# SSD group norm: column sums on four 32-column tiles, a small root and reciprocal, and a broadcast through device memory

## The chip, the cores and the metric

The program runs on one core of a Trainium2 chip. The metric is device time in microseconds (us), from the first to the last instruction with a little around it; the median of three runs is 1379.9 us (1378.26 to 1380.02). Engines: PE (matrix products), ACT, DVE and POOL (elementwise), SP (only issues transfers).

## The reference, cut to what matters

Two layers on 512 tokens of width 1024: a gated short convolution and a Mamba-2 SSD mixer, each followed by a SwiGLU feed-forward. The change lies in the group norm near the end of the SSD mixer: 2048 channels in 8 groups of 256, each token normalised within its group.

```python
def ssd_mixer(h, ...):
    z, xbc, dt_raw = jnp.split(h @ w_in, [M_D_INNER, M_D_INNER + M_CONV_DIM], axis=-1)
    xbc = jax.nn.silu(causal_depthwise_conv(xbc, conv_w) + conv_b)
    ...
    y = ssd_chunked(xs, dt, a, bm, cm) + d_skip.reshape(g, r)[:, :, None] * xs
    y = y.reshape(bsz, s, M_D_INNER) * jax.nn.silu(z)
    y = rms_normalize(y.reshape(bsz, s, g, M_D_INNER // g)).reshape(bsz, s, M_D_INNER) * norm_g
    return y @ w_out
```

`rms_normalize` divides by the root of the mean square plus 1e-6.

## The kernel before

Activations lie transposed, channels on the 128 partitions and the 512 tokens along the row, so one SSD group is two tiles of 128x512. Everything is float32; the large products split each operand into a rounded high part and a low rest and run three products (`mm3`, L259 to L261: high x high, high x low, low x high). `load_w` loads a weight block into `wst`, ACT casts the high part into `whl` (L202) and DVE subtracts to get the low part (L203). There are four `whl` buffers. One projection of 128 columns (`in_chunk`, tile `ip`) is 24 products of 512 columns.

The SSD layer is a software pipeline over the 8 groups. Pass g of the loop (called stage g here, g = 1 to 7) runs the recurrence of group g while it projects group g+1. In code order a stage is:

- projection 1 of group g+1; `step_a` of group g: transposes `xtok` and `btokp`, products `cb`; on DVE `xw`, `xdt` and `cbm`
- projection 2; `step_b`: the states (`st01` at L1051, `st2` at L1053, then `prev` on DVE) and the decays `csb` (exponential on ACT at L1073, multiplication on DVE at L1074)
- projections 3 and 4; `step_cc`: the outputs `yo` and `yd`, gated and squared into `accg`
- two projections for the gate z; then `step_d`, the group norm that is changed

A projection is followed by `conv4`: ACT starts the accumulator `cu` (L954), DVE adds three shifted terms (L957, three instructions), and ACT applies SiLU (L959). In stage 7 there is nothing left to project, and PE begins the output projection (`y`) instead.

The order on PE is the code's, by hand. On DVE, ACT, SP and POOL a scheduler lays the instructions of the loop into one fixed order per engine when the program is built; each engine then works strictly in that order, and an instruction that waits holds up everything behind it. The end of stage g−1 (`step_d` of group g−1) is finished during stage g.

`step_d` before: with a 128x128 matrix of ones PE adds the squares over the partitions, which leaves the same sum in all 128 rows of `ssg`; ACT takes the root of the 128x512 tile `rg` (L1119), DVE its reciprocal (L1120), and two DVE products scale the two tiles `yg` (L1123), in place. The readers of `yg` come later: `y_act` (L1133, L1134) splits it into `ys` for the output projection. `aux_ps` tiles come from one ring of four PSUM buffers in code order, so `st2` takes the buffer that the second `xtok` tile had, once both `xw` and `xdt` have read it. `bt` has two buffers; group g+2 writes the one that group g had.

Of the kernel before, what the change touches and what calls it, by code (L numbers as in the profile page):

```python
# [8 lines left out]
F32 = mybir.dt.float32  # L9
F32R = mybir.dt.float32r  # L10
AF = mybir.ActivationFunctionType
# [5 lines left out]
P = 128  # L17
# [8 lines left out]
NG = 8  # L26
NCH = 4
# [8 lines left out]
def trunk_kernel(  # L36
# [9 lines left out]
    act, dve, pe, pool = nc.scalar, nc.vector, nc.tensor, nc.gpsimd  # L46
# [3 lines left out]
    dram = ctx.enter_context(tc.tile_pool(name="dram", bufs=1, space=DRAM))  # L50

    tmp = ctx.enter_context(tc.tile_pool(name="tmp", bufs=4))
# [7 lines left out]
    def aux_ps(name, shape=(P, T)):  # L60
        return ps.tile(list(shape), F32, tag="aux", name=name, bufs=4)

    def t2(name):
        return tmp.tile([P, T], F32, tag="t2", name=name, bufs=4)
# [4 lines left out]
    ones = consts.tile([P, P], F32, name="ones")  # L69
# [3 lines left out]
    eps_t = consts.tile([P, 1], F32, name="eps")  # L73
# [791 lines left out]
    with ExitStack() as ph:  # L865
# [4 lines left out]

        cs_d = dram.tile([NH, T], F32, name="cs_d")
        ecs_d = dram.tile([NH, T], F32, name="ecs_d")

        dt_tok = consts.tile([P, NH, NCH], F32, name="dt_tok")
        cs_tok = consts.tile([P, NH, NCH], F32, name="cs_tok")
# [89 lines left out]
        class Group:  # L965
# [147 lines left out]
            def step_d(self):  # L1113

                g = self.g
                pt = aux_ps("ssg")
                pe.matmul(pt, ones, self.accg, start=True, stop=True)
                rg = t2("rg")
                act.activation(rg, pt, AF.Sqrt, bias=eps_t, scale=1.0 / 256)  # L1119
                dve.reciprocal(rg, rg)  # L1120
                for q in range(2):
                    y = ygs[2 * g + q]
                    dve.scalar_tensor_tensor(y, y, mng[:, 2 * g + q:2 * g + q + 1], rg, MUL, MUL)  # L1123
# [394 lines left out]
```

## Time and profile before

| | |
|---|---|
| median of three runs | 1379.9 us |
| the profiled execution | 1378.87 us, span 1377.0 us |
| granted TensorE clock, mean over the span | 0.994 |
| ACT busy, POOL busy | 580.2 us (42%), 1.5 us |
| one `ssg` product (L1117), x16 (two passes for each of 8 groups) | 591 ns as recorded |
| root of `rg` (L1119), x8 | 688 ns |
| reciprocal of `rg` (L1120), x8 | 3352 ns |
| scaling of `yg` (L1123), x16 | 745 ns |
| transfers issued by POOL | none |

Columns of the trace's rows: start in us, length in us, engine, line, operation, operands, count, and in brackets the idle time before it with what ended it. PE's records overlap, so what a product costs is read from start to start, not from its length.

### The profile page before, as it was taken

How to read it: one execution, taken by the hardware profiler on the slowest of the kernel's cores; microseconds unless marked ns; L12 is line 12 of the kernel's file. 1: busy time of each engine (PE TensorE's matmuls, PEld its weight loads, DVE VectorE, ACT ScalarE, POOL GpSimd, SP SyncE). 2: the span in 40 equal slices, each digit the busy share in tenths (PEclk: the TensorE clock that was granted, in tenths of full speed). 3: DMA queues.
4: the chain of work that ended last, by engine and by line, in shares of the span. 5: the costliest groups of instructions: out<-in, count | busy, mean ns of one | idle time of the engine just before them, and what ended most of it. 6: DMA issues, size and time to landing. Idle time of an engine off the chain costs nothing.

```text
span 1377.0 us, 17627 instructions
## 1 busy us (share of the span) xinstructions
PE 1353.4 (98%) x6973; PEld 1136.3 (83%) x6973; DVE 911.3 (66%) x1485; ACT 580.2 (42%) x875; POOL 1.5 (0%) x11
## 2 busy tenths in 40 slices
PE   8999999999999999999899999999999999999997
PEld 7788889888888888898778888888889888887886
DVE  5777757478775222669879888787675655334877
ACT  4432247222222211665655656543473222223754
POOL 0000000000000000000000000000000000000000
PEclk9999999999999999999989999999999999999999
DMA  9956670467683322514444324332233986423743
GB/s 314 318 182 218 228 238 24 136 215 274 215 283 106 130 93 69 149 33 144 120 139 128 91 89 138 108 107 92 92 122 134 343 276 244 134 69 128 249 163 118
DMA packets 163702, 222.09 MB, mean 161 GB/s; under 512 B 7060, under 2 KB 112164, under 8 KB 161188
## 3 DMA queue, kind: packets, MB, share of 16 engines
q1 hardware_dynamic: 159616, 208.20, 46.2%
q10 hardware_dynamic: 4004, 12.77, 2.9%
q8 instruction: 55, 0.90, 0.3%
q14 instruction: 27, 0.22, 0.0%
HBM read 207.17 MB, written 13.78 MB: 160 GB/s over the span
## 4 chain that ended last, share of the span: by engine, by line
PE 63%; DVE 3%; DMA 1%; ACT 0%; issue 0%; DVEq 0%; ACTq 0%
PE ip L259 11%; PE ip L261 11%; PE ip L260 11%; PE y L359 5%; PE y L360 5%; PE y L361 5%; PE li L259 2%; PE li L261 2%; PE li L260 2%; PE yd L1089 1%; PE yo L1082 1%; PE pa L1390 1%; PE pa L1391 1%; PE pb L1391 1%; PE pb L1390 1%; PE pb L1389 1%
## 5 line engine op out<-in xcount | busy, mean ns | idle before, releaser
L259 PE MATMUL ip<-h,whl 128*128 128x512 f32 x1096 | 434.6, 397 | 2.7 <-DVE cv L777 2.7
L261 PE MATMUL ip<-h,whl 128*128 128x512 f32 x1096 | 429.4, 392 | 6.6 <-DVE whl L203 6.6
L260 PE MATMUL ip<-h,whl 128*128 128x512 f32 x1096 | 428.4, 391 | 0.0
L261 PEld LDWEIGHTS ip<-h,whl 128*128 128x128 f32 x1096 | 206.8, 189 | 50.9 <-DVE whl L203 7.0
L259 PEld LDWEIGHTS ip<-h,whl 128*128 128x128 f32 x1096 | 206.8, 189 | 47.7 <-issue 5.1
L260 PEld LDWEIGHTS ip<-h,whl 128*128 128x128 f32 x1096 | 206.9, 189 | 43.3 <-issue 1.2
L202 ACT CAST whl<-wst 128x1024 fp32r<-128x1024 f32 (+1 forms) x163 | 152.2, 952 | 200.7 <-PE ip L261 148.2
L203 DVE TENSOR_TENSOR whl<-wst,whl 128x1024 fp32r<-128x1024 f32 (+1 forms) x163 | 177.0, 1102 | 62.4 <-ACT whl L202 62.0
L203 DVE TENSOR_TENSOR whlo<-wsto,whlo 128x1024 fp32r<-128x1024 f32 x46 | 56.3, 1224 | 96.2 <-ACT whlo L202 96.0
L126 DVE SCALAR_TENSOR_TENSOR ada_acc<-ada_st,csil,ada_acc 128x512 f32<-128x512 f32 x140 | 104.8, 749 | 22.6 <-DMA ada_st<-in_ada_w_dram 19.7
L202 ACT CAST whlo<-wsto 128x1024 fp32r<-128x1024 f32 x46 | 48.3, 1050 | 113.8 <-PE y L361 86.7
L259 PE MATMUL li<-h,whl 128*128 128x256 f32 x288 | 83.2, 289 | 0.0
L261 PE MATMUL li<-h,whl 128*128 128x256 f32 x288 | 81.6, 283 | 0.0
L260 PE MATMUL li<-h,whl 128*128 128x256 f32 x288 | 81.5, 283 | 0.0
L957 DVE SCALAR_TENSOR_TENSOR cu<-ip,cols,cu 128x511 f32<-128x511 f32 (+2 forms) x84 | 62.0, 741 | 12.9 <-ACT cu L954 12.7
L359 PE MATMUL y<-whlo,ff 128*128 128x512 f32 x176 | 68.6, 390 | 0.0
L361 PE MATMUL y<-whlo,ff 128*128 128x512 f32 x176 | 68.5, 389 | 0.0
L360 PE MATMUL y<-whlo,ff 128*128 128x512 f32 x176 | 68.5, 389 | 0.0
L259 PEld LDWEIGHTS li<-h,whl 128*128 128x128 f32 x288 | 55.3, 192 | 0.0
L260 PEld LDWEIGHTS li<-h,whl 128*128 128x128 f32 x288 | 55.2, 192 | 0.0
L261 PEld LDWEIGHTS li<-h,whl 128*128 128x128 f32 x288 | 55.1, 191 | 0.0
L359 PE MATMUL y<-whlo,ys 128*128 128x512 f32 x128 | 51.1, 399 | 0.0
(281 smaller groups left out, 1923.5 us busy)
## 6 DMA issues: line engine op xcount, KB each, us to landing
ada_st<-in_ada_w_dram SPq DMA_DIRECT2D x96, 512.0 KB, 5.9
wst<-in_f_w_in_dram SPq DMA_DIRECT2D x44, 1024.0 KB, 7.1
wst<-in_m_w_in_dram SPq DMA_DIRECT2D x14, 1024.0 KB, 5.4
tb<-in_f_w_out_dram SPq DMA_DIRECT2D x22, 512.0 KB, 7.3
td<-tb SPq DMA_DIRECT2D x11, 1024.0 KB, 5.0
wsto<-in_f_w_out_dram SPq DMA_DIRECT2D x10, 1024.0 KB, 4.9
wst<-in_m_w_in_dram SPq DMA_DIRECT2D x20, 512.0 KB, 5.1
wst<-in_a_w_in_dram SPq DMA_DIRECT2D x9, 1024.0 KB, 6.5
```

The costliest lines, as they stand in the source:

```text
L126: dve.scalar_tensor_tensor(acc, w, csil[:, k:k + 1], acc, MUL, ADD)
L202: act.copy(dst[:, 0, :nk, :], src)
L203: dve.tensor_tensor(dst[:, 1, :nk, :], src, dst[:, 0, :nk, :].bitcast(F32), SUB)
L259: pe.matmul(dst, w_at(w, 0, kk), a[:, 0, sl], start=start, stop=False)
L260: pe.matmul(dst, w_at(w, 0, kk), a[:, 1, sl], start=False, stop=False)
L261: pe.matmul(dst, w_at(w, 1, kk), a[:, 0, sl], start=False, stop=stop)
L359: pe.matmul(pst, a[:, 0, tk], wt[:, 0, kk, :], start=k == 0, stop=False)
L360: pe.matmul(pst, a[:, 0, tk], wt[:, 1, kk, :], start=False, stop=False)
L361: pe.matmul(pst, a[:, 1, tk], wt[:, 0, kk, :], start=False, stop=k == K - 1)
L957: dve.scalar_tensor_tensor(u[:, sft:], pst[:, :T - sft], w[3 - sft], u[:, sft:], MUL, ADD)
L1390: pe.matmul(acc[t], a[:, 0, sl], w[1], start=False, stop=False, skip_group_check=True)
L1391: pe.matmul(acc[t], a[:, 1, sl], w[0], start=False, stop=True, skip_group_check=True)
```

## The change

`ssg` becomes a 128x128 tile. Four products, one for each 128 tokens, each use 32 columns of the ones matrix and write their own 32 rows, on four column tiles of the array. The root and the reciprocal then work on 128x128 (tile `r4`) in place of 128x512. Four rows of it, one for each 128 tokens, are stored to device memory as 512 numbers, and a second transfer reads them back into all 128 partitions. Both transfers are issued by POOL. The landing place is the group's own `bt` tile, so `rg` no longer takes one of the four `t2` buffers.

```diff
+        rg_d = [dram.tile([NCH, P], F32, name=f"rg_d{g}") for g in range(NG)]
...
             def step_d(self):
                 g = self.g
-                pt = aux_ps("ssg")
-                pe.matmul(pt, ones, self.accg, start=True, stop=True)
-                rg = t2("rg")
-                act.activation(rg, pt, AF.Sqrt, bias=eps_t, scale=1.0 / 256)
-                dve.reciprocal(rg, rg)
+                pt = aux_ps("ssg", (P, P))
+                for cc in range(NCH):
+                    pe.matmul(pt[cc * 32:(cc + 1) * 32, :], ones[:, :32], self.accg[:, cc * P:(cc + 1) * P],
+                              start=True, stop=True, tile_position=(0, cc * 32))
+                r4 = tmp.tile([P, P], F32, tag="r4", name="r4", bufs=1)
+                act.activation(r4, pt, AF.Sqrt, bias=eps_t, scale=1.0 / 256)
+                dve.reciprocal(r4, r4)
+                pool.dma_start(rg_d[g], r4[0:P:32, :])
+                rg = self.bt
+                pool.dma_start(rg, rg_d[g].rearrange("c t -> (c t)").partition_broadcast(P))
                 for q in range(2):
                     y = ygs[2 * g + q]
                     dve.scalar_tensor_tensor(y, y, mng[:, 2 * g + q:2 * g + q + 1], rg, MUL, MUL)
```

The order on PE stays as it was, with four products of 128 columns where one of 512 stood; lines after the change move down by one to six. The scheduler lays DVE and ACT out anew from stage 1 to the end of the SSD layer. DVE in stage 1 before, from the two `yg` products to the first weight split (`whl`, for projection 3); the reciprocal stands two rows ahead of the first row, and the split for projection 4 two rows behind the last:

```order
L1123 SCALAR_TENSOR_TENSOR yg_5432<-yg_5432,cols_89,rg 128x512
L1123 SCALAR_TENSOR_TENSOR yg_5440<-yg_5440,cols_89,rg 128x512
L957 SCALAR_TENSOR_TENSOR cu<-ip,cols_91,cu 128x510
L957 SCALAR_TENSOR_TENSOR cu<-ip,cols_91,cu 128x511
L957 SCALAR_TENSOR_TENSOR cu<-ip,cols_91,cu 128x509
L957 SCALAR_TENSOR_TENSOR cu<-ip,cols_91,cu 128x510
L1056 TENSOR_TENSOR prev<-prev,dec 128x256
L957 SCALAR_TENSOR_TENSOR cu<-ip,cols_91,cu 128x509
L1058 TENSOR_TENSOR prev<-prev,st_5629 128x256
L1074 TENSOR_TENSOR csb<-csb,cbm 128x1024
L1056 TENSOR_TENSOR prev<-prev,dec 128x256
L203 TENSOR_TENSOR whl<-wst,whl 128x1024
```

DVE at the same place in the changed kernel, where the reciprocal stands three rows ahead of the first row; the last row is the split for projection 4:

```order
L958 SCALAR_TENSOR_TENSOR cu<-ip,cols_91,cu 128x509
L1075 TENSOR_TENSOR csb<-csb,cbm 128x1024
L203 TENSOR_TENSOR whl<-wst,whl 128x1024
L1129 SCALAR_TENSOR_TENSOR yg_5440<-yg_5440,cols_89,bt 128x512
L1129 SCALAR_TENSOR_TENSOR yg_5448<-yg_5448,cols_89,bt 128x512
L958 SCALAR_TENSOR_TENSOR cu<-ip,cols_91,cu 128x511
L1057 TENSOR_TENSOR prev<-prev,dec 128x256
L958 SCALAR_TENSOR_TENSOR cu<-ip,cols_91,cu 128x510
L1059 TENSOR_TENSOR prev<-prev,st_5642 128x256
L958 SCALAR_TENSOR_TENSOR cu<-ip,cols_91,cu 128x509
L1057 TENSOR_TENSOR prev<-prev,dec 128x256
L203 TENSOR_TENSOR whl<-wst,whl 128x1024
```

The first split moved from ten rows behind the `yg` products to the row ahead of them; the second stays behind them, with three `cu` and three `prev` instructions between. Both `yg` now read `bt`, so they wait for the second transfer.

DVE in stage 2 of the changed kernel (stages 3 to 6 differ in that both `xdt`, `cbm` and a second `cu` stand ahead of `yg`):

```order
L1123 RECIPROCAL r_5853<-r_5853 128x128
L203 TENSOR_TENSOR whl<-wst,whl 128x1024
L1024 TENSOR_TENSOR xw<-xtok,dte_tok 128x512
L1026 TENSOR_TENSOR xdt<-xtok,dt_tok 128x512
L958 SCALAR_TENSOR_TENSOR cu<-ip,cols_91,cu 128x511
L1024 TENSOR_TENSOR xw<-xtok,dte_tok 128x256
L1129 SCALAR_TENSOR_TENSOR yg_5769<-yg_5769,cols_89,bt 128x512
L1129 SCALAR_TENSOR_TENSOR yg_5777<-yg_5777,cols_89,bt 128x512
L958 SCALAR_TENSOR_TENSOR cu<-ip,cols_91,cu 128x510
L1026 TENSOR_TENSOR xdt<-xtok,dt_tok 128x512
```

In stage 2 the second `xdt` stands behind the two `yg`, as it did before; what moved ahead of them is a weight split, the first `xdt` and one `cu`. POOL, which had no transfers, now issues these, in pairs, and nothing else stands between them:

```order
L566 MEMSET rows 128x256
masks.py:66 AFFINE_SELECT mask<-mask 128x128
L1124 DMA rg_d_4976<-r_5523 4x128
L1126 DMA bt<-rg_d_4976 128x512
L1124 DMA rg_d_4977<-r_5853 4x128
L1126 DMA bt<-rg_d_4977 128x512
```

`rg_d` is the group's tile in device memory. On POOL the second transfer of a pair waits for the landing of the first.

## Prediction

> **What bounds the kernel.** I read the first part of the page, then the windows view cut at stages of the SSD layer, the chain of waits for the distance from one stage to the next, and the timeline of PE and DVE where a stage is longer.
>
> ```profile
> PE 1353.4 (98%) x6973; PEld 1136.3 (83%) x6973; DVE 911.3 (66%) x1485; ACT 580.2 (42%) x875; POOL 1.5 (0%) x11
> 680.00:720.00 40.00, 33.42 (x164) 27.05 (x163) 32.44 (x54) 23.20 (x28) 0.00 (x0) 0.87 0.40 119
> 720.00:760.50 40.50, 40.50 (x217) 33.77 (x216) 34.87 (x59) 23.77 (x30) 0.00 (x0) 1.00 0.39 117
> 670.13 0.86 PE ssg L1117 x2
> 719.27 0.86 PE ssg L1117 x2
> 759.73 0.86 PE ssg L1117 x2
> ```
>
> PE is busy 1353.4 of 1377.0 us: what PE doesn't execute, or doesn't wait for, is the gain. The windows rows (stage 1, stage 2: length, then PE busy) show stage 2 full, 40.50 of 40.50, and stage 1 with 33.42 of 40.00 at a mean clock of 0.87. By the chain, `ssg` follows `ssg` after 719.27 − 670.13 = 49.1 us in stage 1 and after 759.73 − 719.27 = 40.5 in stage 2. So stage 1 loses 8.6 to 8.7 us, taken as 8.7.
>
> ```profile
> 684.56 0.39 PE L260 MATMUL ip<-h,whl 128*128 128x512 f32 x1
> 691.53 0.79 PE L261 MATMUL ip<-h,whl 128*128 128x512 f32 x1 [6.58 <-DVE whl L203]
> 692.12 0.63 PE L259 MATMUL ip<-h,whl 128*128 128x512 f32 x1
> 696.81 0.61 PE L261 MATMUL ip<-h,whl 128*128 128x512 f32 x1
> 697.96 0.39 PE L259 MATMUL ip<-h,whl 128*128 128x512 f32 x1
> 703.40 0.39 PE L259 MATMUL ip<-h,whl 128*128 128x512 f32 x1
> 678.54 1.23 DVE L1074 TENSOR_TENSOR csb<-csb,cbm 128x1024 f32<-128x1024 f32 x1
> 679.68 3.35 DVE L1120 RECIPROCAL rg<-rg 128x512 f32<-128x512 f32 x1
> 683.51 1.41 DVE L1123 SCALAR_TENSOR_TENSOR yg<-yg,cols,rg 128x512 f32<-128x512 f32 x2
> 684.84 2.71 DVE L957 SCALAR_TENSOR_TENSOR cu<-ip,cols,cu 128x510 f32<-128x510 f32 x4
> 690.25 1.22 DVE L203 TENSOR_TENSOR whl<-wst,whl 128x1024 fp32r<-128x1024 f32 x1
> 678.93 1.98 ACT L202 CAST whl<-wst 128x1024 fp32r<-128x1024 f32 x2
> ```
>
> PE (first six rows) stops in projection 3: the third product waits 6.58 us for the low part of a weight block. Then eleven steps from 692.12 to 696.81 take 0.43 us each, where the 24 from 697.96 to 703.40, a whole projection in 5.44 us, take 0.227. DVE (next five) is late with that split (690.25) because by its order the reciprocal (3.35 us), two `yg` and two convolutions come first, though ACT (last row) had cast both blocks of the pair by 680.9.
>
> **The products.** The same shape, 128 rows by 32 columns, 128 moving columns, float32 on four column tiles, runs at the start of the kernel, between full-width products. One float32 product has two records.
>
> ```profile
> 19.72 0.40 PE L714 MATMUL li<-h,whl_b 128*128 128x512 f32 x1
> 20.05 1.08 PE L184 MATMUL ada_pe<-ada_st,rows 128*32 128x128 f32 x32
> 21.06 0.96 PE L714 MATMUL li<-h,whl_b 128*128 128x512 f32 x3
> 31.38 1.95 PE L184 MATMUL ada_pe<-ada_st,rows 128*32 128x128 f32 x64
> 33.26 0.44 PE L191 MATMUL ada_pe<-ident,ada 128*128 128x128 f32 x2
> 706.26 1.90 PE yd L1089 x32
> 708.15 0.43 PE ip L259
> ```
>
> Start to start, 32 records take 21.06 − 20.05 = 1.01 us and 64 take 1.88: 0.027 a record, plus 0.14 that doesn't scale. A further 0.1 stands ahead of the group, which starts 0.33 behind the product at 19.72, not 0.23. Eight records then cost 8 × 0.027 + 0.24 = 0.46 us, where the two passes of the old `ssg` cost 0.86 by the chain: −0.40, eight times −3.2 us. The outer ends: −5.2 if entering and leaving the tiles costs nothing (8 × 0.65), and +1.9 if the four don't overlap (0.86 + 0.24 each).
>
> The rows of `yd`, two 64-column tiles, show the cost of leaving: the product behind them takes 0.43 in the chain, 0.2 more than the pitch. The Trainium skill (TensorEngine Tiling, Key Properties) says that changing the tiling mode drains the engine, which speaks against four small products between full ones; the row agrees. By that page's up-to-fourfold speedup alone `ssg` would fall to a quarter, the −5.2 end, and the sum would be 2 us lower than with the drain.
>
> **Root and reciprocal.**
>
> ```profile
> L935 ACT ACTIVATE csb<-csb 128x128 f32<-128x128 f32 x1 | 0.3, 311 | 0.7 <-DVE csb L933 0.7
> L908 DVE RECIPROCAL cs_tok<-cs_tok 128x128 f32<-128x128 f32 x1 | 1.0, 952 | 0.0
> 721.61 0.69 ACT L1119 ACTIVATE rg<-ssg,eps 128x512 f32<-128x512 f32 x1
> 762.98 0.69 ACT L1119 ACTIVATE rg<-ssg,eps 128x512 f32<-128x512 f32 x1
> ```
>
> On 128x128, ACT takes 0.31 us (an exponential of that size, row one) where the root takes 0.69 (the last two rows, stages 2 and 3), and DVE 0.95 where the reciprocal took 3.35. That is 3 us of ACT and 19 us of DVE in all, but off PE's path except in stage 1, so it counts only there. Elsewhere I cost it at nothing: PE's own work covers it, full in stage 2. Without that cover the 19 us would show in full.
>
> **The two transfers.** POOL waits for the reciprocal, issues the store, waits for its landing, issues the load; DVE waits for that at the first `yg`, with everything behind it in its order. Call R the time from the end of the reciprocal to the landing. No row shows a transfer issued by POOL; the nearest are these (KB, median us from issue to landing), and the share of the transfer engines is zero at both places where R runs.
>
> ```profile
> out_dram<-x SPq DMA_DIRECT2D x8, 256.0 KB, 2.0
> cs_d<-csb SPq DMA_DIRECT2D x1, 64.0 KB, 3.1
> ea<-in_m_a_log_dram SPq DMA_DIRECT2D x1, 16.0 KB, 2.8
> r<-td SPq DMA_DIRECT2D x11, 256.0 KB, 3.5
> ecsb<-ecs_d ACTq DMA_DIRECT2D x16, 256.0 KB, 5.9
> 680.00:684.00 4.00, 4.00 (x20) 3.35 (x19) 4.00 (x3) 1.67 (x2) 0.00 (x0) 1.00 0.00 0
> 720.00:724.00 4.00, 4.00 (x19) 3.29 (x18) 1.67 (x1) 3.95 (x5) 0.00 (x0) 1.00 0.00 0
> ```
>
> The store lies between 2.0 (an output tile) and 3.1 (also a table to device memory); the load between 2.8 (a small broadcast) and 5.9 (256 KB broadcast, but queued behind 1 MB). With idle engines I take the upper store, the quiet 256 KB load at 3.5 and 0.4 for two hand-overs: R = 7.0. Ends: 4.8 and 9.0, and above it what POOL may add.
>
> **Stage 1 with the new order.** PE is 0.4 earlier by the shorter `ssg`, and so is DVE, which waits for PE ahead of this place. The reciprocal starts at 679.68 − 0.4 = 679.3 and ends at 680.2. Three `cu` (0.66 each), one `csb` (1.14, from 678.54 to 679.68) and the split (1.13: its 1.22 less the 0.09 by which DVE's records overlap) end at 684.5. PE asks for it at 684.56 + 0.23 − 0.4 = 684.4: the 6.58 us are gone but for 0.1. That removes 8.7 − 0.1. What is late next is the split for projection 4. Behind `yg` (1.33, from 683.51 to the row at 684.84) come three `cu`, three `prev` (0.34 each) and the split, so it ends at 680.2 + R + 1.3 + 2.0 + 1.0 + 1.1 = 685.6 + R. PE asks 24 products later: 684.5 + 5.44 = 690.0. The wait is R − 4.4, or 2.6 us at R = 7.0. The weights of the z projections are split behind that and needed two projections later.
>
> A wait of that size also halves the clock:
>
> ```profile
> 64.39 0.47 PE L259 MATMUL ip<-h,whl 128*128 128x512 f32 x1 [2.69 <-DVE cv L777]
> 65.87 0.63 PE L259 MATMUL ip<-h,whl 128*128 128x512 f32 x1
> 68.86 0.56 PE L260 MATMUL ip<-h,whl 128*128 128x512 f32 x1
> ```
>
> After 2.69 us idle the seven products from 65.87 to 68.86 took 0.43 each, a loss of about 1.6 us with the next. I add 1.6 for a wait near 2.6 and 2.6 for one above 5 (thirteen slow products at 691.53); under 2 nothing. Stage 1 then gains 8.7 − 0.1 − 2.6 − 1.6 = 4.4 us; at R = 4.8 it gains 8.2, at 9.0 some 2.0 (wait 4.6, clock 2.0).
>
> **The other stages.**
>
> ```profile
> 733.89 0.59 PE L1053 MATMUL st<-xw,btok 128*128 128x256 f32 x2
> ```
>
> In stage 2 the root ends at 721.61 + 0.31 and the reciprocal at 722.8 (0.09 of it overlapped). `yg`, one `cu` and the second `xdt` end at 725.4 + R, and `st2`, in that `xdt`'s PSUM buffer, starts at 733.89 + 0.15 − 0.4: hidden to R = 8.2. In stages 3 to 6 (root from 762.98, so the reciprocal ends at 764.2) the next that PE needs behind `yg` is the split for projection 4: `cu`, two `csb` and it end at 769.6 + R; PE asks 20.8 us after `ssg` at 759.73, an estimate from stage 2 (`st2` ends at 734.5, projection 3 takes 5.44). Hidden to R = 10.9. `bt` is wanted by the group after next, some 20 us later, and stage 7 works ahead by up to five `ys` buffers; both count as nothing. The kernel's end keeps its distance, since PE is full behind the layer.
>
> **Sum.** Products −3.2, stage 1 −4.4, transfers elsewhere 0: −7.6 against the profiled 1378.87: 1371.3. The median of the runs is 1.0 above that execution, so 1372.3; I forecast 1372.
>
> **Rivals** (by the median, with −3.2 for the products).
>
> - A short trip, R = 4.8: the split for projection 4 is 0.4 late, the clock holds, 1379.9 − 3.2 − 8.2 = 1368.5. Idle transfer engines speak for it, the wait of one engine on another twice over against. The Trainium skill (DMA: Bandwidth & Descriptors, Anatomy of one DMA) gives about 2.0 us a transfer plus bytes at 436 GB/s: 4.6 us for the pair, an estimate, so this case; no row here shows a POOL transfer.
> - A trip above 11 us, and slower: then `yg` holds DVE in every stage. At R = 12.5, stage 1 loses 8.1 + 2.6 against the prize of 8.7, stage 2 loses 4.3 and stages 3 to 6 lose 1.6 each: 8.7 − 10.7 − 0.1 − 4.3 − 6.4 + 3.2 = −9.6, so 1389. It decides from R = 11, where the sum is near zero. The longest row is 5.9 + 3.1 = 9.0; POOL would have to add 2 us.
> - A trip of 9 to 11: stage 1's gain shrinks to nothing and stage 2 waits up to 2.8 us: 1376 to 1380.
> - The four products don't run side by side: +1.9 in place of −3.2, 1377.4. The rows at 20.05 speak against it.
>
> **Numbers.** Forecast (R from 5.5 to 9, 1369 to 1376) 0.55; short trip 0.22; 9 to 11 us 0.10; above 11 us 0.09; no overlap of the products 0.04. A measurement of this kernel tells about 0.2% (2.8 us) from no change, so faster means below 1377.1. Faster is the first two and a third of the third: 0.80, less 0.02 for what I don't see, 0.78; same 0.11 from the rest of the third and the last; slower 0.11. The range from 1366 to 1380 takes in the short trip with the upper end of the products (1368.5 − 2.0) and the trip of 11 us.
>
> **What would show it.** Right: the wait of PE for `whl` at projection 3 is gone and a shorter one, 1 to 5 us, stands at projection 4 of stage 1 with a half-clock stretch behind it; `ssg` near 0.46 us in the chain; stages of 40.1 us; DVE idle at `yg` for the transfer in every stage. Wrong: R far from 7 (read from the reciprocal's end to `yg`), PE waits in stages 2 to 6, or `ssg` at 0.9 us.

## The result, and the profile after

| | before | after |
|---|---|---|
| median of six runs each | 1379.96 us | 1372.32 us (1368.89 to 1373.76) |
| the profiled execution, span | 1378.87, 1377.0 us | 1371.87, 1370.1 us |

The ratio is 0.9943, with a 95% interval from 0.9931 to 0.9955: 7.6 us faster, against a forecast of 1372. The total came out as forecast; the terms did not, and the rest of this document explains why.

First the page of the changed kernel, PE's busy row and the group that carried the wait, then the chain of waits, its rows for `ssg` (stages 1, 2, 3 and the last):

```profile
PE 1349.0 (98%) x7021; PEld 1133.1 (83%) x7021; DVE 894.9 (65%) x1485; ACT 577.3 (42%) x875; POOL 10.8 (1%) x27
L261 PE MATMUL ip<-h,whl 128*128 128x512 f32 x1096 | 428.0, 391 | 1.6 <-DVE whl L203 1.5
...
671.18 0.36 PE ssg L1119 x8
712.64 0.36 PE ssg L1119 x8
752.78 0.36 PE ssg L1119 x8
...
958.96 0.36 PE ssg L1119 x8
```

PE waits 1.5 us for `whl` in place of 6.6. Stage 1 is 712.64 − 671.18 = 41.46 us (before 49.14), stage 2 40.14 (before 40.46). From the first `ssg` to the last it is 287.78 us, before 298.01 (670.13 to 968.14): the layer gained 10.2 us, not the forecast 7.6. Ahead of it this execution was 1.05 us later (in 13 profiles of all kernels here the first `ssg` starts anywhere from 668.7 to 671.2, so that is chance). Behind it, it lost: 1370.1 − 958.96 = 411.1 us against 408.9. The sum is −10.2 + 1.05 + 2.3 = −6.9, the difference of the two spans.

Stage 1 of the changed kernel, by the timeline of DVE, POOL and PE:

```profile
680.41 0.95 DVE L1123 RECIPROCAL r<-r 128x128 f32<-128x128 f32 x1
681.27 2.22 DVE L958 SCALAR_TENSOR_TENSOR cu<-ip,cols,cu 128x511 f32<-128x511 f32 x3
683.41 1.22 DVE L1075 TENSOR_TENSOR csb<-csb,cbm 128x1024 f32<-128x1024 f32 x1
684.54 1.22 DVE L203 TENSOR_TENSOR whl<-wst,whl 128x1024 fp32r<-128x1024 f32 x1
687.43 1.42 DVE L1129 SCALAR_TENSOR_TENSOR yg<-yg,cols,bt 128x512 f32<-128x512 f32 x2 [1.68 <-DMA bt<-rg_d]
...
691.74 1.22 DVE L203 TENSOR_TENSOR whl<-wst,whl 128x1024 fp32r<-128x1024 f32 x1
681.68 0.71 POOL L1124 DMA_DIRECT2D rg_d<-r  x1 [679.59 <-DVE r L1123]
684.04 0.56 POOL L1126 DMA_DIRECT2D bt<-rg_d  x1 [1.65 <-PE ip L261]
685.81 0.50 PE L261 MATMUL ip<-h,whl 128*128 128x512 f32 x1
693.00 0.50 PE L261 MATMUL ip<-h,whl 128*128 128x512 f32 x1 [1.46 <-DVE whl L203]
693.34 0.39 PE L259 MATMUL ip<-h,whl 128*128 128x512 f32 x1
693.57 0.39 PE L260 MATMUL ip<-h,whl 128*128 128x512 f32 x1
```

The split for projection 3 (684.54) now stands behind the short reciprocal, three `cu` and one `csb`, and PE goes on at 685.81, some 0.3 us late. The trip R runs from 681.36 to `yg` at 687.43: 6.07 us. The split for projection 4 (691.74) comes behind it, and PE waits 1.46 us. Behind that wait the steps are 0.34 and then 0.23 us: the clock was not halved.

The end of the program, before and after: the chain's row for the first load of the last FFN, and PE's products behind it.

```profile
1258.91 4.83 DMA r<-td
```
```profile
1249.27 5.04 DMA r<-td
1255.43 0.50 PE L1395 MATMUL pb<-w,a 128*128 128x512 f32 x1 [0.75 <-ACT w L1330]
1256.69 0.56 PE L1396 MATMUL pb<-w,a 128*128 128x512 f32 x1 [0.76 <-DVE w L1331]
1257.05 0.63 PE L1397 MATMUL pb<-w,a 128*128 128x512 f32 x1
1257.48 0.63 PE L1395 MATMUL pb<-w,a 128*128 128x512 f32 x1
...
1260.04 0.57 PE L1395 MATMUL pz<-w,a 128*128 128x512 f32 x1
```

The load lands 0.2 us later, two waits of 0.75 us follow (0.54 and 0.76 before), and then seven steps of 0.43 us. From the first `pa` product to the end the program took 116.9 us, before 114.2. Of these 2.7 us, 0.2 are the load and 1.2 the slow steps. Another 1.2 lie behind PE's last product, which starts 7.4 us ahead of the end before and 8.6 after. The order of the instructions of this stretch is the same in both kernels on every engine.

### The profile page after: what moved, and what is told of

It is laid out like the page before. It is cut to its first block, busy times and chain, and to the rows that moved or that the text cites. A ratio compares the mean times of both kernels' runs of the same rounds, so it can differ in the third digit from the quotient of the medians.

```text
span 1370.1 us, 17791 instructions
## 1 busy us (share of the span) xinstructions
PE 1349.0 (98%) x7021; PEld 1133.1 (83%) x7021; DVE 894.9 (65%) x1485; ACT 577.3 (42%) x875; POOL 10.8 (1%) x27
## 4 chain that ended last, share of the span: by engine, by line
PE 64%; DVE 2%; DMA 1%; ACT 0%; issue 0%; SPq 0%; DVEq 0%; ACTq 0%
PE ip L259 11%; PE ip L261 11%; PE ip L260 11%; PE y L359 5%; PE y L361 5%; PE y L360 5%; PE li L259 2%; PE li L261 2%; PE li L260 2%; PE yd L1090 1%; PE yo L1083 1%; PE pb L1396 1%; PE pb L1397 1%; PE pz L1395 1%; PE pz L1397 1%; PE pz L1396 1%
## 5 line engine op out<-in xcount | busy, mean ns | idle before, releaser
L202 ACT CAST whlo<-wsto 128x1024 fp32r<-128x1024 f32 x46 | 48.4, 1051 | 113.6 <-PE y L361 86.8
```

Source lines behind the costliest of these rows:

```text
L202: act.copy(dst[:, 0, :nk, :], src)
```

## Experiments

The kernels ran in three groups (four, four and the three shifts), each on one chip beside the kernel before, whose medians were 1378.79, 1378.96 and 1378.69 us. Stage 1 is the distance of the first two `ssg` in the profiled execution.

| | median, us | ratio to before, 95% interval | stage 1, us |
|---|---|---|---|
| after_again | 1370.31 | 0.9941 [0.9928, 0.9954] | 41.62 |
| order_only | 1374.33 | 0.9969 [0.9956, 0.9981] | 46.40 |
| order_after | 1368.58 | 0.9925 [0.9913, 0.9937] | 39.30 |
| full_sums | 1378.33 | 0.9992 [0.998, 1.0003] | 48.98 |
| order_full | 1374.82 | 0.9967 [0.995, 0.9983] | 42.04 |
| quarter_recip | 1375.56 | 0.9976 [0.9965, 0.9987] | 45.69 |
| long_trip | 1372.70 | 0.9951 [0.9934, 0.9968] | 42.33 |
| double_products | 1368.64 | 0.9914 [0.9894, 0.9935] | 40.66 |
| shift_before | 1381.47 | 1.002 [1.0008, 1.0033] | 48.62 |
| shift_after | 1369.51 | 0.9929 [0.991, 0.9949] | 41.60 |
| shift_best | 1365.66 | 0.9906 [0.9887, 0.9925] | 39.28 |

**What gained in stage 1: the order on DVE, or less work for it?**

order_only, the old arithmetic with another order. `step_e` is the second half of `step_d` (reciprocal and `yg`; the other groups still run it there), `splits` lists DVE's weight splits as they are written, and `issue_after` lets an engine issue what stands in its block only after the instruction named:

```diff
...
+                    if g == 1 and i == 2:       # in the loop, behind projections 3 and 4
+                        with tc.issue_after(splits[-1].ins):
+                            first.step_e()      # group 0: reciprocal and yg
```

> The kernel before, with the old sums, root and reciprocal; only in stage 1 DVE's reciprocal and the two scalings of group 0 are queued behind both weight splits of projections 3 and 4. PE's order and the order of SP's transfers stay as before. Theory 'order' (the 8.7 us of stage 1 were the place of the split behind 3.35 us of reciprocal and what followed it): no wait of PE for whl in stage 1, the distance from ssg to ssg there 40.5 us instead of 49.1, 1379.96 - 8.6 = 1371.4 us, so as fast as the changed kernel. Theory 'work' (DVE must have less to do: 2.4 us less reciprocal in each stage): the delayed reciprocal only moves the wait to a later projection, stage 1 stays at 46 to 49 us, 1377 to 1380 us.

```profile
688.04 3.35 DVE L1129 RECIPROCAL rg<-rg 128x512 f32<-128x512 f32 x1
...
700.88 1.22 DVE L205 TENSOR_TENSOR whl<-wst,whl 128x1024 fp32r<-128x1024 f32 x1
702.15 0.79 PE L263 MATMUL ip<-h,whl 128*128 128x512 f32 x1 [3.95 <-DVE whl L205]
```

My theory 'order' fell as I had put it. The waits at projections 3 and 4 are gone, but 3.95 us stand at the first z projection, whose split (700.88) is behind the delayed reciprocal, `yg` and step c. Stage 1 is 46.40, within what 'work' said; the median, 1374.33, lies between what the two theories said (1371.4, and 1377 to 1380). So I took the z split ahead as well, order_full:

```diff
...
+                        if g == 1 and q == 2:
+                            with tc.issue_after(splits[-1].ins):
+                                first.step_e()
+                    if g == 1 and i == 2:
+                        nxt.weights(2)
+                        with tc.issue_after(splits[-2].ins):
+                            step()              # step_cc behind the first z split
```

> The kernel before with its old sums, root and reciprocal, as in order_only, and in stage 1 also the first z split taken ahead of step c on DVE (in order_only PE waited 3.95 us for that split, which stood behind the delayed reciprocal, the scalings and step c). Theory 'order' (DVE's work fits into stage 1, only its order is at fault): the z split ends near 697.9, PE asks at 698.2, no wait of PE for whl; stage 1 39.6 us (39.30 of order_after plus 0.32 for the products), 1378.8 - 9.5 - 0.6 = 1368.7 us. Theory 'work' (old reciprocals don't fit, 4.7 us of reciprocal and scalings must show somewhere): a wait of 2 us or more appears at the end of stage 1 (ssg for accg, or the next xtok), stage 1 43 us or more, 1372 us or more.

```profile
712.83 1.10 PE L1119 MATMUL ssg<-accg,ones 128*128 128x512 f32 x2 [2.17 <-DVE accg L1112]
714.04 0.63 PE L262 MATMUL ip<-h,whl 128*128 128x512 f32 x1
```

The wait for `whl` shrank to 0.2 us, and 2.17 us came up at the end of the stage, `ssg` for `accg`, with half-clock steps (0.43) behind it: the place that 'work' named. Stage 1, 42.04, fits neither theory's number (39.6, and 43 or more); the median, 1374.82, fits 'work'. Stages 1 and 2 together took 84.34 us. Without waits they would take 39.30 (order_after) + 0.32 (the dearer products) + 40.46 = 80.1, so order alone brought 5.2 of the 9.5 us that stage 1 had lost, and the other order that I tried, order_only, brought less there (86.86 us for the two stages). The medians of the two fell by 4.5 and 4.1, order_only's more. Then less work alone, quarter_recip, which leaves the other three quarters of `rg` without a reciprocal:

```diff
-                dve.reciprocal(rg, rg)
+                dve.reciprocal(rg[:, :P], rg[:, :P])
```

> The kernel before, with the reciprocal taken of only the first 128 of 512 columns (the other three quarters are left as the root): DVE has 2.4 us less in each stage, and no transfer moves the scalings back. By its order the split for projection 3 still stands behind the scalings, six cu, one csb and three prev: 679.7 + 0.9 + 1.3 + 4.0 + 1.1 + 1.0 + 1.1 = 689.2 against 691.4 before. Theory 'order': the wait of PE falls from 6.6 to 4.4 us only, stage 1 46.8 us, 1378.8 - 2.3 - 0.6 = 1375.9 us. Theory 'work' (the shorter reciprocal carries the gain): wait under 1 us, stage 1 near 41 us, 1371 us.

```profile
690.07 0.50 PE L261 MATMUL ip<-h,whl 128*128 128x512 f32 x1 [4.20 <-DVE whl L203]
```

A wait of 4.20 us where the sum of what stands ahead of the split gave 4.4, and a median of 1375.6 where it gave 1375.9. Stage 1, 45.69, is 1.1 below the 46.8 that I had said. Size alone brings 49.14 − 45.69 = 3.4 us. And the trip alone, with old sums and old reciprocal, full_sums:

```diff
+                pt = aux_ps("ssg")
+                pe.matmul(pt, ones, self.accg, start=True, stop=True)
+                r4 = t2("r4")
...
+                pool.dma_start(rg_d[g].rearrange("c t -> (c t)").unsqueeze(0), r4[0:1, :])
```

> The changed kernel with the old full-width sums, root on 128x512 and reciprocal on 128x512 (3.35 us), but still with the trip by way of device memory (one row stored, broadcast back). Theory 'order': with the longer reciprocal the split for projection 3 stands by DVE's order behind six cu, one csb and the scalings, which wait for the trip: 683.0 + 6.1 + 1.3 + 0.3 + 1.1 = 691.9 against PE's asking at 684.8, a wait near 7.1 us with a half-clock stretch behind it; stage 1 49 to 51 us, 1380 to 1382 us. Theory 'trip reorders' (any wait for a transfer pushes the scalings behind the split, and the small root and reciprocal matter little): stage 1 stays near 42 to 44 us and only the products are lost, 1372.3 + 2.6 = 1375 to 1377 us.

```profile
690.74 0.79 PE L261 MATMUL ip<-h,whl 128*128 128x512 f32 x1 [7.12 <-DVE whl L203]
```

The wait was forecast at 7.1 from DVE's order and the durations in it, and measured 7.12. The median, 1378.33, is 2 us below what I had said, and stage 1, 48.98, just under my 49 to 51; the median is not told apart from before. The trip by itself gains nothing: the longer DVE work puts the split behind `yg` again.

The answer is both. The split is late by the durations that stand ahead of it in DVE's order; the short reciprocal takes 2.4 us off them, and with the trip besides, the scheduler puts the split ahead of `yg`. Neither did it alone (quarter_recip, full_sums). That the scheduler does so because it sees `yg` wait for a transfer is my reading; no run shows its reason.

**What is left in stage 1.** order_after is the change, with the scalings of group 0 behind both splits and a landing place of their own:

```diff
+                rg = self.bt if g else t2("rgb")
...
+                    if g == 1 and i == 2:
+                        with tc.issue_after(splits[-1].ins):
+                            first.step_e()      # group 0: yg
```

> The changed kernel; in stage 1 alone the scalings of group 0 are queued on DVE behind both splits, and the broadcast lands in a buffer of its own. Theory 'order': the wait of 1.46 us at projection 4 goes, stage 1 falls from 41.46 to 40.15 us, the median from 1372.3 to 1371.0 us, and where that wait had halved the clock in some execution, by up to 1.6 us more. Rival (the wait at projection 4 is the landing of its weights, not the place behind the scalings): no change, 1372.3 us.

> The changed kernel again, beside the others. Both theories: 1372.3 us, stage 1 41.5 us, trip of the transfers 6.1 us in stage 1. Of interest is how often the last stretch of the program (ssg of stage 8 to the end, 408.9 us before, 411.1 after) has a half-clock stretch: if that stretch belongs to the change it stays at 411; if it is chance it goes back to about 409.

```profile
669.79 0.36 PE ssg L1121 x8
709.09 0.36 PE ssg L1121 x8
```

No wait for `whl` is left, and stage 1 takes 39.30 us, 2.3 less than in after_again on the same chip; the median is 1.7 us lower. So the wait at projection 4 was the place behind `yg`. That 39.30 is below 40.15 I had not expected: stage 1 is shorter by itself than the other stages. From `ssg` to `ssg` PE has 136 projection products in it and 144 in each of stages 2 to 6, because the first `ssg` stands behind eight products of projection 1. A wait of 0.71 us for `cb`, which stage 1 has before and after, goes against that. The tail of after_again stayed long (115.8 us from the first `pa`), so it was not chance in one execution.

long_trip adds a hop:

```diff
...
-                pool.dma_start(rg_d[g], r4[0:P:32, :])
+                pool.dma_start(rg_e[g], r4[0:P:32, :])
+                pool.dma_start(rg_d[g], rg_e[g])
```

> The changed kernel with one more hop between the store and the broadcast (device memory to device memory), so the trip is 6.1 + 2.4 = 8.5 us. The prediction's step (each us of trip above 4.4 is a us of wait at projection 4, and a half-clock stretch above 2.5 us): a wait of 1.46 + 2.4 = 3.9 us, 2 us of half clock, stage 1 46 us, 1374.5 us. Theory 'the order moves with the trip': in DVE's new order three cu and two prev of stage 1 stand ahead of the scalings and not behind, so the split for projection 4 ends at 681.4 + 8.5 + 1.3 + 0.3 + 1.1 = 692.6 as in the changed kernel (692.9): wait 1.2 to 1.5 us, stage 1 41.5 us, 1370.3 us.

```profile
689.55 1.41 DVE L1131 SCALAR_TENSOR_TENSOR yg<-yg,cols,bt 128x512 f32<-128x512 f32 x2 [2.00 <-DMA bt<-rg_d]
691.22 1.22 DVE L203 TENSOR_TENSOR whl<-wst,whl 128x1024 fp32r<-128x1024 f32 x1
692.49 0.50 PE L261 MATMUL ip<-h,whl 128*128 128x512 f32 x1 [2.32 <-DVE whl L203]
692.83 0.39 PE L259 MATMUL ip<-h,whl 128*128 128x512 f32 x1
```

The trip became 9.56 us (reciprocal to `yg`), 1.1 more than I had worked out. The wait is 2.32: not the 5.2 that the fixed order would give (9.56 − 4.4), but 0.9 more than in the changed kernel. 'The order moves with the trip' had 1.2 to 1.5 us for a trip of 8.5; the 1.1 us on top make 2.3 to 2.6. So 3.5 us more of trip than in the changed kernel (9.56 against 6.07) cost 0.9 in stage 1 and nothing in stages 2 to 6 (40.14 to 40.15 each). From the last `ssg` to the first `pa` it is 1.3 us longer than in the changed kernel; there the last group's trip took 11.52 us, against 9.07. And 2.32 us of wait did not halve the clock.

**The products.** double_products runs the four twice:

> The changed kernel with the four 32-column products run twice in a row (the second set into a buffer of its own, which the root reads). The prediction's price (0.027 us a record, 0.24 for entering and leaving): the second set adds 8 x 0.027 = 0.22 us, stages 40.36 us, +1.7 us in all. Rival (each group of four pays its own entry, or the four don't overlap): 0.54 us or more a set, stages 40.7 us, +4.3 us.

```profile
711.05 0.36 PE ssg L1119 x8
751.45 0.36 PE ssg L1119 x8
691.40 0.50 PE L261 MATMUL ip<-h,whl 128*128 128x512 f32 x1 [0.51 <-DVE whl L203]
```

The stages are 40.40 us, 0.25 more than with one set: the price is by the record, 0.03 each, and the set of four enters and leaves the tiles once. The kernel is not slower for its 2 us of extra products, 1368.64: with them the scheduler laid out DVE so that the split for projection 4 starts at 690.13 and PE waits 0.51 us (last row), and its tail is short (113.5 us).

**The tail.** From the first `pa` to the end the four profiles so far with 7021 PE records (after, after_again, order_after, long_trip) took 115.8 to 116.9 us, the others (6973 or 7085) 113.1 to 114.2. The page's DMA part for the 5 us ahead of the first `pa` shows what differs. Here are the changed kernel and, in the second fence, double_products:

```profile
q1 hardware_dynamic: 274, 0.77, 50.5%
q8 instruction: 1, 0.02, 1.4%
```
```profile
q1 hardware_dynamic: 337, 0.99, 64.4%
```

A block of instructions is loaded (0.02 MB, one packet) beside the first loads of `r`. The page after counts 55 such packets on q8, 0.90 MB, one for about 255 of PE's 14,042 products and weight loads. The change adds 96 of those, so every later block boundary moves. In the kernel before, the block came 13 us behind `pa`. To move it on purpose I changed idle products at the start of the program, at PE's first wait:

```diff
-            busy(idle, 10)
+            busy(idle, 3)
+            for _ in range(31):
+                pe.matmul(idle[:8, :8], ident[:, :8], ident[:, :8], start=True, stop=True)
```

> The kernel before with 48 more PE records at the very start: of ten idle products on 128x128 three are kept and 31 of 8x8 put in for seven (same stretch of time), so that every later PE instruction stands 96 places further, as in the changed kernel by its 48 more records. In the four profiles with 7021 PE records one PE instruction block is loaded 4 to 5 us ahead of the last FFN's first pa, beside the first r loads, which land after 5.0 to 5.2 us; in the five with 6973 and the one with 7085 it is loaded 11 to 14 us behind it, and the same load lands after 4.0 to 4.8. Theory 'instruction block': here the block falls ahead of pa, the load lands after 5.0 us or more, and from the first pa to the end the program takes 115.8 to 116.9 us in place of 113.1 to 114.2: about +2 us, 1380.9 against 1378.9. Rival (the slower tail comes from something else that the change does): no change, 1378.9 us, tail 114.

> The changed kernel with the same 48 more records at the start. Theory 'instruction block': the block is loaded some 17 us earlier, clear of the r loads; they land after 4.0 to 4.8 us, from the first pa to the end 113.1 to 114.2 us in place of 115.8 to 116.9, 1370.3 - 2 = 1368.3 us. Rival: no change, 1370.3 us.

> The kernel of order_after (scalings of group 0 behind both splits) with the same 48 more records at the start. Theory 'instruction block': 1368.6 - 2 = 1366.6 us, stage 1 39.3 us, first pa to the end 113.1 to 114.2 us. Rival: no change, 1368.6 us.

The chain's row for the same load in the three, in this order, and the q8 row of the first; the other two have none in that window:

```profile
1256.90 6.46 DMA r<-td
q8 instruction: 1, 0.02, 2.7%
```
```profile
1248.02 4.03 DMA r<-td
```
```profile
1245.22 4.34 DMA r<-td
```

In shift_before the block falls 3 us ahead of `pa`, the load takes 6.46 us, PE waits 2.2 us for it at half clock behind, and the tail grows from 114.2 to 119.8 us; the whole is 2.8 us slower with the arithmetic of before. In shift_after and shift_best the block is 14 us ahead (some 9 us earlier than without the shift, not the 17 that I had said), the load takes 4.03 and 4.34, and the tail 113.4 and 113.6. The medians go the same way for shift_best (1365.66, 2.9 below order_after) and less for shift_after (0.8 below after_again, where I had said 2); these pairs ran in different groups, and the intervals of both overlap. Shown is that the slow load goes with the place of the block: 5.04 to 6.46 us in the five profiles where it comes 3 to 5 us ahead of `pa`, 4.01 to 4.83 in the other eight, and three of the 13 were moved on purpose. How one packet delays that load isn't shown.

The first load is only part of the longer tail. after_again, which has no slow steps there, takes 1.6 us longer than the kernel before from the first `pa` to the end; 0.2 of that stand at the first load, and 1.2 behind PE's last product. What differs there is how long SP takes to issue the last eight weight blocks `t` (before, then after):

```profile
1338.97 10.19 SPq L1378 DMA_DIRECT2D t<-td  x8
1330.67 11.38 SPq L1384 DMA_DIRECT2D t<-td  x8
```

In the four profiles a later block falls among these issues, 85 to 86 us behind `pa`. They then take 11.4 to 11.7 us, the longest wait of ACT for `t` is 4.4 to 5.6, and 8.5 to 8.6 us follow the start of PE's last product. In the other nine no block falls there: 10.2 us, 3.9 to 4.0, and 7.1 to 8.2. The shifts moved both blocks at once, so how the gain of shift_after and shift_best divides between the two places isn't shown.

shift_best, with the order and the shift, is the fastest kernel here: 13 us below the kernel before, where the change alone had 8.5 (after_again).

## Why the prediction was right, point by point

The total was right by luck, because two errors cancelled: the layer gained 2.6 us more than the sum, and the tail, which the sum left alone, gave 2.3 back in the profiled execution (1.1 in after_again, whose median is 8.5 us below the kernel before).

- **Products: −3.2 forecast, −2.6 measured.** The stages without waits are 0.32 us shorter, not 0.40. The set costs 0.54 where I had 0.46: 0.25 for the eight records (I had 0.22) and 0.29 for entering and leaving (I had 0.24). The rows at the kernel's start gave the right form. That changing the tiling drains the engine, as the Trainium skill says (TensorEngine Tiling (Array Packing), Key Properties), agrees with the 0.29.
- **What stage 1 had lost: 8.7 forecast, 9.5 measured.** The step that failed took the length of stage 2 for that of stage 1 without waits, though stage 1 has eight projection products fewer, in the kernel before too.
- **R: 7.0 forecast, 6.07 measured in stage 1** (6.9 to 7.6 in stages 2 to 7 and 9.07 behind the last group). The store landed after 1.7 us and the load after 4.3 (medians). The Trainium skill (DMA: Bandwidth & Descriptors, Anatomy of one DMA) had led to an estimate of 4.6 for the pair; the trace is 1.5 above that in its shortest case, so the short-trip rival fell.
- **The wait at projection 4, R − 4.4:** 1.67 with the measured R, and 1.46 measured. The step was right. For another R it would not have been: the scheduler's order, which I held fixed, moves with the trip. In long_trip the trips of stages 2 to 6 took 10.0 to 11.0 us and cost nothing, so the rivals' prices for long trips were too high there.
- **The clock, +1.6 forecast, none measured.** "A wait of that size also halves the clock" rested on one row, and for the 1.46 that came the forecast's own bound, under 2 nothing, held. 2.32 us didn't (long_trip), 2.17 (order_full) and 2.69 did, and two waits of 0.75 in the tail did in one execution and not in another. The Trainium skill (TensorE: Matmul & The Clock Gate, Part 1) has a free-running window of about 3.4 us and a clock that drops after an idle one. That the length alone doesn't decide agrees with a free-running window; but waits well below 3.4 us halved it here, and the measurement decides.
- **Stage 1 in all: 4.4 forecast, 7.4 measured** beside the products: 0.8 from the base, 1.1 from the shorter wait, 1.6 from the clock, less about 0.5 for steps of 0.34 and 0.52 at the two waits that I had left out.
- **Stages 2 to 6 hide the trip:** right, 40.14 to 40.15 us each. Two of them had been 0.3 us longer before (`ssg` for `accg`); in order_only and full_sums, with the old reciprocal, they were not, so I don't put that down to the change.
- **"The kernel's end keeps its distance":** wrong. With the added PE instructions, instruction blocks are loaded beside the first and the last loads of the last FFN.

## What to carry to other kernels

On an engine that works strictly in order, a late operand is late by the sum of what stands ahead of it: write that list down from the order and add the durations, and here the wait came out within 0.2 us twice (4.4 against 4.20, 7.1 against 7.12). Then ask of any change that adds or removes a wait how it lays out that list anew, because the gain can be had by order, by size, or only by both. And when a change adds or drops instructions on an engine, look at stretches that it doesn't touch: compare them between landmarks, and try the same kernel with a few harmless instructions at the start before the difference is put down to the change.

## What the runs showed of the hardware

- One packet of 0.02 MB on q8 comes for about every 255 PE instructions. Where one came 3 to 5 us ahead of the last FFN's first `pa`, that FFN's first load took 5.04 to 6.46 us and the stretch behind `pa` 115.8 to 119.8; elsewhere they took 4.01 to 4.83 and 113.1 to 114.2.
- A POOL transfer of 2 KB takes 0.6 to 0.7 us to issue and lands after 1.7; the broadcast load of 256 KB lands after 4.3, and the pair with its hand-overs takes 6.07 to 9.07 us.
- Waits of PE of 2.17 and 2.69 us, and once two of 0.75, were followed by steps of 0.43 us in place of 0.23; waits of 1.46 and 2.32 us, and two of 0.75 in another execution, were not.
